# RMSNorm and swish: squares of three rows in one ScalarE operation, summed by one VectorE operation, eps on GpSimd

## The chip, the cores and the metric

The kernel runs on one core of a Trainium2 chip. The metric is the device time of a run in microseconds (us); medians of several runs are given. The profiled span is about 1.9 us shorter than that time (161.1 against 163.01 in the kernel before). All runs told of here are in the same, fast state, with a granted clock of 1.0. The experiments ran in three sets on three chips, and the kernel before ran beside each set (medians 163.10, 163.04 and 163.09 us); so between sets the ratio to the kernel before is compared, and not a few tenths of a us.

## The reference

```python
batch, seq, dim = 16, 1024, 512          # x: float32, gamma: ones, eps: 1e-5
rms = np.sqrt(np.mean(x ** 2, axis=-1, keepdims=True) + eps)
x_norm = x / rms * gamma
return (x_norm * (1.0 / (1.0 + np.exp(-x_norm)))).astype(np.float32)
```

There are 16384 rows of 512 numbers: 33.55 MB come in and 33.55 MB go out.

## The kernel before

Rows lie 128 at a time on the partitions. A chunk is four rows per partition (128x2048 numbers, 1 MB); there are 32 chunks in 11 tiles, and one tile is one load and one store of 4, 8 or 16 rows per partition. The ring holds 96 rows, so most loads are asked for long before the data is used.

```python
sizes = [4, 4, 8] + [16] * 6 + [8, 8];  ring = 96;  cn = 4;  n_act = 3

def sums(k):                    # sum of squares of each row
    for j in range(cn):
        row = xb[:, chunks[k] + j, :]
        if j < n_act:           # three rows on ScalarE
            nc.scalar.activation(out=junk[:], in_=row, func=AF.Square,
                                 accum_out=ms[:, k, j : j + 1])
        else:                   # the fourth on VectorE
            nc.vector.tensor_tensor_reduce(out=junk[:], in0=row, in1=row, ...,
                                           accum_out=ms[:, k, j : j + 1])
def root(k):                    # (sum / 512 + eps) ** -0.5
    nc.vector.tensor_scalar(out=aeps[:, k, :], in0=ms[:, k, :], scalar1=inv_d, scalar2=eps_f, ...)
    nc.gpsimd.tensor_tensor(out=rstd[:, k, :], in0=aeps[:, k, :], in1=neg_half[:], op=ALU.pow)
def norm(k):                    # four VectorE operations of 128x512, in place
    ...
def swish(k):                   # one Silu of 128x2048 on ScalarE, in place
    ...
for k in range(K + 3):          # order of issue on every engine
    sums(k); root(k); (store of a tile whose chunks are all <= k-3); norm(k - 1); swish(k - 2); (loads)
```

(Cut: `...`, the names of the junk tiles, and the bounds on k.)

## Time and profile before

| | before |
|---|---|
| time, median (range) | 163.01 us (162.89 to 163.02) |
| span | 161.1 us |
| busy: VectorE, ScalarE, GpSimd | 110.7, 118.7, 46.4 us |
| moved | 67.1 MB, 417 GB/s over the span |
| last store issued | at 146.8 us |

The lines, and how they are read, are in the prediction.

### The profile page before, as it was taken

To read this page: it belongs to the slowest core of one execution; us is meant where nothing else is said; L and a number is where in the kernel's file an instruction comes from. 1 tells how busy PE (TensorE), PEld (TensorE's weight loads), DVE (VectorE), ACT (ScalarE), POOL (GpSimd) and SP (SyncE) were. 2 spreads that over 40 slices of the span, in tenths; PEclk is the share of its full clock that TensorE was granted. 3 is DMA by queue.
4 is the path that set the end of the run, shared out by engine and by line. 5 is a ranking of instruction groups with operands and counts; after the bars stand their busy time and mean duration, and the time that the engine had idled before them with its cause. 6 is when DMAs were issued, how large, how long until landed. Compare 5 with 4: busy or idle time off the path is not lost.

```text
span 161.1 us, 612 instructions
## 1 busy us (share of the span) xinstructions
DVE 110.7 (69%) x226; ACT 118.7 (74%) x225; POOL 46.4 (29%) x38
## 2 busy tenths in 40 slices
DVE  0376946998999999999966998069999604990000
ACT  3447919999999999999939996099999408954000
POOL 1052403333444433333333333033333302400000
DMA  5999989999899999999999999999999999999993
GB/s 171 437 435 521 390 352 488 413 403 480 366 407 431 484 411 447 399 456 447 399 447 456 399 439 464 417 415 421 431 435 464 419 403 472 415 415 423 439 415 146
DMA packets 3180, 67.15 MB, mean 417 GB/s; under 512 B 356, under 2 KB 356, under 8 KB 360
## 3 DMA queue, kind: packets, MB, share of 16 engines
q1 hardware_dynamic: 1584, 33.56, 49.1%
q10 hardware_dynamic: 1592, 33.56, 48.4%
q14 instruction: 4, 0.03, 0.0%
HBM read 33.56 MB, written 33.55 MB: 417 GB/s over the span
## 4 chain that ended last, share of the span: by engine, by line
DMA 59%; ACT 20%; another core or an unknown queue 4%; issue 4%; DVE 3%; SPq 1%; DVEq 0%; ACTq 0%
DMA xb<-in_x_dram 41%; DMA out_dram<-xb 19%; ACT junk_a L80 12%; ACT xb L111 8%; DVE xb L104 3%; SPq L70 1%; DVEq L178 0%; DVE aeps L93 0%; ACTq L80 0%
## 5 line engine op out<-in xcount | busy, mean ns | idle before, releaser
L104 DVE SCALAR_TENSOR_TENSOR xb<-xb,rstd,gamma_sb 128x512 f32<-128x512 f32 x128 | 87.4, 745 | 0.0
L80 ACT ACTIVATE junk_a<-xb 128x512 bf16<-128x512 f32 x96 | 59.0, 615 | 23.9 <-DMA xb<-in_x_dram 23.9
L97 POOL TENSOR_TENSOR rstd<-aeps,neg_half 128x4 f32<-128x4 f32 x32 | 45.6, 1426 | 94.1 <-DVE aeps L93 94.1
L111 ACT ACTIVATE xb<-xb 128x2048 f32<-128x2048 f32 x32 | 60.7, 1896 | 1.8 <-DVE xb L104 1.8
L86 DVE CUSTOM_DVE_ANT_0 junk_v<-xb 128x512 bf16<-128x512 f32 x32 | 21.9, 685 | 19.6 <-DMA xb<-in_x_dram 19.6
L80 ACT ACTIVATION_READ_ACCUMULATOR junk_a<-xb 128x1 f32 x96 | 18.0, 187 | 0.0
L93 DVE TENSOR_SCALAR aeps<-ms 128x4 f32<-128x4 f32 x32 | 5.4, 170 | 14.5 <-ACT junk_a L80 14.5
L117 ACT ACT_TABLE_LOAD x1 | 1.3, 1283 | 2.4 <-issue 2.4
L86 DVE DVE_READ_ACCUMULATOR2_ANT ms<- 128x1 f32 x32 | 2.6, 82 | 0.0
L140 DVE STREAM_SHUFFLE gamma_sb<-gamma 128x512 f32<-128x512 f32 x1 | 0.7, 725 | 0.0
L114 POOL MEMSET gamma<- 128x512 f32 x1 | 0.5, 524 | 0.3 <-POOLq L164 0.3
L164 POOL MEMSET const-float32-0.0<- 128x1 f32 x1 | 0.1, 98 | 0.2 <-issue 0.2
L164 POOL MEMSET const-bfloat16-1.0<- 128x1 bf16 x1 | 0.1, 101 | 0.0
L164 POOL MEMSET const-uint8-127<- 128x1 uint8 x1 | 0.1, 101 | 0.0
L115 POOL MEMSET neg_half<- 128x4 f32 x1 | 0.1, 101 | 0.0
L164 POOL MEMSET const-float32-1.0<- 128x1 f32 x1 | 0.1, 98 | 0.0
L140 DVE LOAD_MASK_SELECT gamma_sb<-gamma x1 | 0.0, 14 | 0.0
## 6 DMA issues: line engine op xcount, KB each, us to landing
xb<-in_x_dram SPq DMA_DIRECT2D x6, 4096.0 KB, 43.8
out_dram<-xb ACTq DMA_DIRECT2D x6, 4096.0 KB, 34.6
xb<-in_x_dram SPq DMA_DIRECT2D x3, 2048.0 KB, 38.8
out_dram<-xb ACTq DMA_DIRECT2D x3, 2048.0 KB, 13.9
xb<-in_x_dram SPq DMA_DIRECT2D x2, 1024.0 KB, 5.8
out_dram<-xb ACTq DMA_DIRECT2D x2, 1024.0 KB, 19.7
gamma<-in_gamma_dram ACTq DMA_DIRECT2D x1, 8.0 KB
```

The costliest lines, as they stand in the source:

```text
L70: nc.sync.dma_start(out=buf(t), in_=dram(xf, t))
L80: nc.scalar.activation(out=junk[:], in_=row, func=AF.Square, accum_out=ms[:, k, j : j + 1],)
L86: nc.vector.tensor_tensor_reduce(out=junk[:], in0=row, in1=row, scale=1.0, scalar=0.0, op0=ALU.mult, op1=ALU.add, accum_out=ms[:, k, j : j ...
L93: nc.vector.tensor_scalar(out=aeps[:, k, :], in0=ms[:, k, :], scalar1=inv_d, scalar2=eps_f, op0=ALU.mult, op1=ALU.add,)
L97: nc.gpsimd.tensor_tensor(out=rstd[:, k, :], in0=aeps[:, k, :], in1=neg_half[:], op=ALU.pow)
L104: nc.vector.scalar_tensor_tensor(out=row, in0=row, scalar=rstd[:, k, j : j + 1], in1=gamma_sb[:], op0=ALU.mult, op1=ALU.mult,)
L111: nc.scalar.activation(out=rows, in_=rows, func=AF.Silu)
L114: nc.gpsimd.memset(gamma4[:], 0.0)
L115: nc.gpsimd.memset(neg_half[:], -0.5)
L117: nc.scalar.preload_act_table_set("silu_and_others")
L140: nc.vector.stream_shuffle(gamma_sb[:], gamma4[:], [0] * 32)
L164: nc = _bacc.Bacc("TRN2", target_bir_lowering=False, num_devices=1)
```

## The change

The intent is to take fixed costs away: three squares of 615 ns become one operation, their three accumulator reads of 187 ns become one VectorE sum, and the small operation with eps (170 ns) leaves VectorE. (In the kernel before a ScalarE operation on 512 elements lasts 615 ns and one on 2048 lasts 1896; the straight line through the two has some 190 ns left at 0 elements.) In exchange ScalarE takes over the fourth row, and the factor 1/512 moves into the scale of the squares. The diff is shortened, with `...` for what was cut; the pool `squares_pool` and `at = chunks[k]` are set up above it.

```diff
 def sums(k):
-    for j in range(cn):
-        ... Square with accumulator on ScalarE (j < 3), square-and-sum on VectorE (j = 3)
+    sq = squares_pool.tile([P, n_sq, D], fp32, name="sq")        # PSUM, two buffers, n_sq = 3
+    nc.scalar.activation(out=sq[:], in_=xb[:, at : at + n_sq, :], func=AF.Square, scale=inv_d**0.5)
+    for j in range(n_sq, cn):                                    # the fourth row
+        nc.scalar.activation(out=junk[:], in_=xb[:, at + j, :], func=AF.Square,
+                             scale=inv_d**0.5, accum_out=ms[:, k, j : j + 1])
+    nc.vector.tensor_reduce(out=ms[:, k, 0:n_sq], in_=sq[:], op=ALU.add, axis=X)
 def root(k):
-    nc.vector.tensor_scalar(out=aeps[:, k, :], in0=ms[:, k, :], scalar1=inv_d, scalar2=eps_f, ...)
+    nc.gpsimd.tensor_scalar(out=aeps[:, k, :], in0=ms[:, k, :], scalar1=eps_f, op0=ALU.add)
     nc.gpsimd.tensor_tensor(out=rstd[:, k, :], in0=aeps[:, k, :], in1=neg_half[:], op=ALU.pow)
```

More of the change, by code (lines that the diff above doesn't have):

```diff
@@ L33 @@
     cn = 4
-    n_act = 3
+    n_sq = 3
     N = sum(sizes)
@@ L48 @@
     pool = ctx.enter_context(tc.tile_pool(name="all", bufs=1))
+    squares_pool = ctx.enter_context(
+        tc.tile_pool(name="squares", bufs=2, space=bass.MemoryType.PSUM)
+    )
     junk_pool = ctx.enter_context(tc.tile_pool(name="junk", bufs=1))
@@ L75, in sums @@
     def sums(k):
-        for j in range(cn):
-            row = xb[:, chunks[k] + j, :]
-            if j < n_act:
-                junk = junk_pool.tile([P, D], bf16, name=f"junk_a{j}")
-                nc.scalar.activation(
-                    out=junk[:], in_=row, func=AF.Square,
-                    accum_out=ms[:, k, j : j + 1],
-                )
-            else:
-                junk = junk_pool.tile([P, D], bf16, name=f"junk_v{j}")
-                nc.vector.tensor_tensor_reduce(
-                    out=junk[:], in0=row, in1=row,
-                    scale=1.0, scalar=0.0, op0=ALU.mult, op1=ALU.add,
-                    accum_out=ms[:, k, j : j + 1],
-                )
+        at = chunks[k]
+        sq = squares_pool.tile([P, n_sq, D], fp32, name="sq")
+        nc.scalar.activation(
+            out=sq[:], in_=xb[:, at : at + n_sq, :], func=AF.Square,
+            scale=inv_d**0.5,
+        )
+        for j in range(n_sq, cn):
+            junk = junk_pool.tile([P, D], bf16, name=f"junk_a{j}")
+            nc.scalar.activation(
+                out=junk[:], in_=xb[:, at + j, :], func=AF.Square,
+                scale=inv_d**0.5, accum_out=ms[:, k, j : j + 1],
+            )
+        nc.vector.tensor_reduce(
+            out=ms[:, k, 0:n_sq], in_=sq[:], op=ALU.add,
+            axis=mybir.AxisListType.X,
+        )
     def root(k):
-        nc.vector.tensor_scalar(
-            out=aeps[:, k, :], in0=ms[:, k, :], scalar1=inv_d, scalar2=eps_f,
-            op0=ALU.mult, op1=ALU.add,
+        nc.gpsimd.tensor_scalar(
+            out=aeps[:, k, :], in0=ms[:, k, :], scalar1=eps_f, scalar2=None,
+            op0=ALU.add,
         )
```

## The prediction

> **What bounds the kernel now.** I read the page from the top: busy shares, the row of slices, the chain that ended last, the groups; then the stretches at the end and the timeline of one steady chunk. A chunk is 4 rows per partition (128x2048 elements, 1 MB); there are 32 of them, in 11 tiles.
>
> ```profile
> span 161.1 us, 612 instructions
> DVE 110.7 (69%) x226; ACT 118.7 (74%) x225; POOL 46.4 (29%) x38
> DMA  5999989999899999999999999999999999999993
> HBM read 33.56 MB, written 33.55 MB: 417 GB/s over the span
> DMA xb<-in_x_dram 41%; DMA out_dram<-xb 19%; ACT junk_a L80 12%; ACT xb L111 8%; DVE xb L104 3%; SPq L70 1%; DVEq L178 0%; DVE aeps L93 0%; ACTq L80 0%
> ...
> L104 DVE SCALAR_TENSOR_TENSOR xb<-xb,rstd,gamma_sb 128x512 f32<-128x512 f32 x128 | 87.4, 745 | 0.0
> L80 ACT ACTIVATE junk_a<-xb 128x512 bf16<-128x512 f32 x96 | 59.0, 615 | 23.9 <-DMA xb<-in_x_dram 23.9
> L97 POOL TENSOR_TENSOR rstd<-aeps,neg_half 128x4 f32<-128x4 f32 x32 | 45.6, 1426 | 94.1 <-DVE aeps L93 94.1
> L111 ACT ACTIVATE xb<-xb 128x2048 f32<-128x2048 f32 x32 | 60.7, 1896 | 1.8 <-DVE xb L104 1.8
> L86 DVE CUSTOM_DVE_ANT_0 junk_v<-xb 128x512 bf16<-128x512 f32 x32 | 21.9, 685 | 19.6 <-DMA xb<-in_x_dram 19.6
> ```
>
> The reader sees a DMA row at 9 in nearly every slice but the first and the last, while no engine is over 74% busy and both VectorE and ScalarE end their idle time by waiting for loads (19.6 and 23.9 us). The kernel moves 67.1 MB; that is the bound. The windows of the end, with the columns window, length, busy time and count of DVE, ACT, POOL, clock, DMA share, GB/s:
>
> ```profile
> 61.00:105.00 44.00, 34.70 (x72) 35.77 (x69) 14.39 (x10) 1.00 1.00 433
> 134.00:147.00 13.00, 9.26 (x18) 10.93 (x16) 2.88 (x2) 1.00 1.02 441
> 147.00:161.10 14.10, 0.00 (x0) 0.00 (x0) 0.00 (x0) 1.00 0.79 339
> ```
>
> The transfers run at about 433 GB/s to the end, and the last 14.1 us hold no compute at all: the last store is issued at 146.8 us and then only the queue of stores drains. So compute could end later without moving the end, by an amount that I work out below. It is the number on which this case turns.
>
> The timeline of a steady chunk, start and length in us:
>
> ```profile
> 43.74 1.90 ACT L111 ACTIVATE xb<-xb 128x2048 f32<-128x2048 f32 x1
> ...
> 47.38 1.90 ACT L111 ACTIVATE xb<-xb 128x2048 f32<-128x2048 f32 x1
> ```
>
> From one Silu to the next it is 3.64 us: ScalarE sets the pace of compute where loads are there. The DMA needs 2.1 MB per chunk, read and written, or 4.84 us at 433 GB/s, so compute is 1.2 us per chunk ahead of the DMA.
>
> [...] In the trace the square-and-sum of 512 lasts 685 ns but its accumulator read starts 0.61 us after it[...]. No PSUM operand is in this trace. [...] All 128 normalizations last 743 to 752 ns, most power operations beside them: VectorE, at least, pays nothing here. [...]
>
> **The change part by part, for one chunk.**
>
> ScalarE. Removed: three squares of 512 with accumulator reads, which pace at 0.61 us each (from the timeline: 42.52, 43.13, 43.74), 1.84 us. Added: one square of 1536, [...] 1.37 us, and one square with accumulator, 0.61 us: 1.98 us. With the Silu at 1.80 us of pace the chunk is 3.78 us against 3.64: ScalarE gets 0.14 us slower, since it takes over the fourth row and saves only two fixed costs. [...]
>
> VectorE. Removed: the square-and-sum (0.61 us of pace plus 0.08 for its read) and the mean-plus-eps of 0.09 us pace: about 0.78 us. Added: one sum of 3x512 from PSUM, [...] I take 1.72 us. Staying: four normalizations, each 0.66 us after the one before (two of them, 745 ns long, merge to 1.41 us), 2.65 us. Sum: 2.65 + 1.72 = 4.37 us, against 3.43 before. **VectorE replaces ScalarE as the pace of compute**, with 32 x 4.37 = 140 us of a 161 us span. But 4.37 is still under the 4.84 us of the DMA.
>
> GpSimd. Added: an addition of eps on 128x4; no such row exists, so I bound it by the power's 1.43 us. From the end of a chunk's sum to its first normalization VectorE does four normalizations and a sum in the new order of instructions (2.65 + 1.72 = 4.37 us). Two GpSimd operations and their signals take at most 2 x 1.43 + some 0.3 = 3.2 us. It fits, 1.2 us to spare. The scale of 1/512 folded into the square is free.
>
> DMA: the same loads and stores in the same order.
>
> **Does the slower VectorE reach the end?** Tile 3 lands at 23.6 us (the timeline shows ScalarE starting chunk 4 at 23.70), so chunk 4's sum starts at 23.7 + 1.4 = 25.1 us. From there VectorE runs 4.37 us per chunk: later loads landed at 84.5 (chunk 20), 104.8 (24) and 133.7 (30), and the sums of these chunks start at 95.0, 112.5 and 138.7, so it never waits for a load again. Then:
> - sum of chunk 31 starts at 25.1 + 27 x 4.37 = 143.1, two chunks' normalization follow: 143.1 + 1.7 + 2 x 2.65 = 150.1, the last Silu 1.9: last store issued at 152.0 us instead of 146.8.
> - Silu of chunk 27, which releases tile 8's store: the sum of 28 starts at 130.0, + 1.7 + 2.65 + 1.9 = 136.3 us (before: 133.9).
>
> How late may they be? After 134 us the windows show 13.0 x 441 + 14.1 x 339 = 10.5 MB. The three last stores are 8.4 MB of these, so 2.1 MB of older stores remain at 134 and last till 134 + 4.9 = 138.9. Tile 8's store needs its first bytes by then: 136.3 + about 1.5 = 137.8. Margin 1 us. The last store (2.1 MB) is reached at 134 + 19.4 = 153.4; its first bytes come at 152.0 + 1.5 = 153.5. Margin none. (The 1.5 is an estimate: a 1 MB load took 4.8 us from issue to landing, of which 2.4 are transfer at 433 GB/s, the other 2.4 lie ahead and behind.) So the span should just hold, 161 to 161.5, and the time with it, 163.2 us. Every 0.05 us on VectorE's chunk beyond this adds 27 x 0.05 = 1.4 us.
>
> **The rivals.**
> 1. The sum costs more than 1.72 us[...]. Then VectorE is the bound: at 1.80 the last store is 2 us late and the time about 165, at 1.90 about 167.5. For it: no row of the kernel measures it. [...]
> 2. GpSimd takes over: if addition and power need over 4.3 us, each chunk is longer by the excess, some 2.8 us per 0.1. For it: the power is already 1.43 us for 4 elements. Against: the first power, before any normalization, took only 1.01.
> 3. Compute gets faster and the kernel with it: nothing speaks for it. Even free compute leaves 67.1 MB at 433 GB/s, 155 us, plus the first landing and the last receipt; the DMA row has no gap to fill.
> 4. Fully hidden[...]: 163.0.
>
> **Range and chances.** Rivals 4 and the middle case give 163.0 to 163.5 (some 70%); a reduction 0.05 to 0.1 us slower gives 164 to 166 (20%); the rest is worse. Faster by 2% would need under 159.8: 1%. Slower by 2% is over 166.3, a chunk of about 4.5 us: 9%. Range 162.6 to 165.6, point 163.2.
>
> **What would show it.** VectorE busy about 142 us and with hardly any idle time after chunk 4; the sum's row at 1.7 to 1.8 us; ScalarE waiting about 0.6 us per chunk for normalizations instead of for loads; the last store issued near 152 us; the DMA row at 9 until the last slices. Wrong, if the DMA row thins out after slice 33, or if the normalization waits for GpSimd.

Passages that no trace or run of this case shows are cut, with the cut marked, and terms of the forecast's sum are among them: how the 1.37 us of the square of 1536 and the 1.72 us of the sum were come by. The sum came to 2.65 + 1.72 = 4.37 us for VectorE's chunk and 1.37 + 0.61 + 1.80 = 3.78 us for ScalarE's, and from 4.37 to a last store at 152.0 us and a time of 163.2 us. The 1.37 can be had from the trace: the straight line through 615 ns at 512 elements and 1896 at 2048 gives 1469 ns at 1536, less the 0.10 us by which a Silu's length (1.90) is above its pace (1.80). For the 1.72 there is nothing of the kind, since no row of the kernel before reads PSUM or sums as many elements: it was the author's estimate. So were the some 0.3 us for GpSimd's signals; the timeline of the changed kernel below has 0.16 us from the end of the sum to the addition and 0.09 us from the addition to the power. That the scale is free is what the run shows: squares of 512 last 613 ns with it and 615 without. That the transfers can't go above 433 GB/s was not shown.

## The result, and the profile after

The changed kernel took 162.64 us (162.43 to 162.95), against 163.01 of the kernel before: ratio 0.9981, 95% interval 0.9962 to 0.9999. (A ratio is the mean time of one kernel's fast runs over that of the other's fast runs of the same rounds, so it is not quite the ratio of the medians.)

The page of the changed kernel: busy time, the DMA row, the chain that ended last by engine, and the groups (operation, shapes, count, busy us, mean ns, idle time before and what ended it).

```profile
DVE 139.1 (86%) x162; ACT 126.2 (78%) x129; POOL 63.2 (39%) x70
DMA  5999989899899999999999999899999999999994
DVE 74%; DMA 13%; issue 2%; ACT 2%; SPq 1%; DVEq 1%
...
L108 DVE SCALAR_TENSOR_TENSOR xb<-xb,rstd,gamma_sb 128x512 f32<-128x512 f32 x128 | 87.2, 743 | 0.0
L115 ACT ACTIVATE xb<-xb 128x2048 f32<-128x2048 f32 x32 | 61.1, 1909 | 14.1 <-DVE xb L108 14.0
L91 DVE TENSOR_REDUCE ms<-sq 128x3 f32<-128x1536 f32 x32 | 56.0, 1749 | 9.5 <-ACT sq L81 9.4
L81 ACT ACTIVATE sq<-xb 128x1536 f32<-128x1536 f32 x32 | 46.0, 1439 | 7.8 <-DMA xb<-in_x_dram 7.8
L97 POOL TENSOR_SCALAR aeps<-ms 128x4 f32<-128x4 f32 x32 | 18.4, 575 | 79.1 <-DVE ms L91 79.1
L101 POOL TENSOR_TENSOR rstd<-aeps,neg_half 128x4 f32<-128x4 f32 x32 | 44.0, 1376 | 2.7
```

VectorE grew by 28.4 us and ScalarE by 7.5 us, and the time did not follow: the DMA row is as full as before. ScalarE's waits for loads fell from 23.9 to 7.8 us, and a wait of 14.0 us for VectorE's normalizations took their place. The page's chain now names VectorE for 74% of the span. It follows the last store back through the chunks; whether that makes VectorE the bound is what the experiments ask.

The timeline of one chunk of the changed kernel (start, length, engine, operation):

```profile
42.27 1.75 DVE L91 TENSOR_REDUCE ms<-sq 128x3 f32<-128x1536 f32 x1
43.94 2.73 DVE L108 SCALAR_TENSOR_TENSOR xb<-xb,rstd,gamma_sb 128x512 f32<-128x512 f32 x4
44.18 0.58 POOL L97 TENSOR_SCALAR aeps<-ms 128x4 f32<-128x4 f32 x1 [2.26 <-DVE ms L91]
...
44.85 1.39 POOL L101 TENSOR_TENSOR rstd<-aeps,neg_half 128x4 f32<-128x4 f32 x1
...
46.59 1.75 DVE L91 TENSOR_REDUCE ms<-sq 128x3 f32<-128x1536 f32 x1
```

A chunk takes VectorE 46.59 - 42.27 = 4.32 us, without a gap: 1.67 from the start of the sum to the first normalization and 2.65 for the four. The windows of the end (columns as in the prediction):

```profile
134.00:147.00 13.00, 13.00 (x17) 9.75 (x10) 5.92 (x6) 1.00 1.03 444
147.00:160.90 13.90, 1.56 (x3) 2.77 (x2) 0.00 (x0) 1.00 0.80 342
```

Compute now reaches into the last stretch (1.56 and 2.77 us, where there was none), and the transfers move the same as before, 444 and 342 GB/s against 441 and 339. The last store was issued at 150.5 us instead of 146.8.

### The profile page after: what moved, and what is told of

Same layout as the page of the kernel before. It is cut to its first block, busy times and chain, and to the rows that moved or that the text cites. A ratio compares the mean times of both kernels' runs of the same rounds, so it can differ in the third digit from the quotient of the medians.

```text
span 160.9 us, 488 instructions
## 1 busy us (share of the span) xinstructions
DVE 139.1 (86%) x162; ACT 126.2 (78%) x129; POOL 63.2 (39%) x70
## 4 chain that ended last, share of the span: by engine, by line
DVE 74%; DMA 13%; issue 2%; ACT 2%; SPq 1%; DVEq 1%
DVE xb L108 45%; DVE ms L91 29%; DMA xb<-in_x_dram 13%; ACT xb L115 1%; ACT sq L81 1%; SPq L73 1%; DVEq L182 1%; DVEq L108 0%
## 5 line engine op out<-in xcount | busy, mean ns | idle before, releaser
L91 DVE TENSOR_REDUCE ms<-sq 128x3 f32<-128x1536 f32 x32 | 56.0, 1749 | 9.5 <-ACT sq L81 9.4
L81 ACT ACTIVATE sq<-xb 128x1536 f32<-128x1536 f32 x32 | 46.0, 1439 | 7.8 <-DMA xb<-in_x_dram 7.8
L97 POOL TENSOR_SCALAR aeps<-ms 128x4 f32<-128x4 f32 x32 | 18.4, 575 | 79.1 <-DVE ms L91 79.1
L101 POOL TENSOR_TENSOR rstd<-aeps,neg_half 128x4 f32<-128x4 f32 x32 | 44.0, 1376 | 2.7
L87 ACT ACTIVATE junk_a<-xb 128x512 bf16<-128x512 f32 x32 | 19.6, 613 | 0.0
L87 ACT ACTIVATION_READ_ACCUMULATOR junk_a<-xb 128x1 f32 x32 | 6.0, 186 | 0.0
```

What stands on the lines that cost most here:

```text
L81: nc.scalar.activation(out=sq[:], in_=xb[:, at : at + n_sq, :], func=AF.Square, scale=inv_d**0.5,)
L87: nc.scalar.activation(out=junk[:], in_=xb[:, at + j, :], func=AF.Square, scale=inv_d**0.5, accum_out=ms[:, k, j : j + 1],)
L91: nc.vector.tensor_reduce(out=ms[:, k, 0:n_sq], in_=sq[:], op=ALU.add, axis=mybir.AxisListType.X,)
L97: nc.gpsimd.tensor_scalar(out=aeps[:, k, :], in0=ms[:, k, :], scalar1=eps_f, scalar2=None, op0=ALU.add,)
```

## The experiments

**Theory A**: both kernels sit on the floor of the transfers, and compute may end later by a certain slack before the stores run dry. **Theory B**: the VectorE chain sets the end, as the chain's 74% suggests, and the gain elsewhere cancels the loss. **Theory C**: compute has ample room, whatever it costs. (The diffs are shortened: arguments and the new small tiles that they write to are left out.)

### Doses: one, two and four small VectorE operations more in each chunk

```diff
         nc.vector.tensor_reduce(out=ms[:, k, 0:n_sq], in_=sq[:], ...)
+        for i in range(n):                                        # n = 1, 2, 4
+            nc.vector.tensor_scalar(out=dose[:, k, i, :], in0=neg_half[:], scalar1=1.0, op0=ALU.add)
```

> The changed kernel with one extra VectorE operation on 128x4 per chunk, about 0.08 us, which nobody waits for. Theory A (DMA bound; compute may end 1.3 us later than the 150.5 us of the changed kernel before the stores run dry): VectorE's chunk 4.32 -> 4.40 us, last store issued at 150.5 + 27 x 0.08 = 152.7, time 162.6 + 0.9 = 163.5 us. Theory B (the VectorE chain that the changed kernel's page names for 74% of the span sets the end): the whole 27 x 0.08 = 2.2 us is added, 164.8. Theory C (DMA alone, compute has ample room): 162.6.

> The same with two extra operations, about 0.16 us per chunk. A: last store at 154.9, of which 1.3 us are absorbed, time 162.6 + 3.1 = 165.7. B: 162.6 + 4.4 = 167.0. C: 162.6.

> The same with four, about 0.33 us per chunk. A: last store at 159.5, time 162.6 + 7.6 = 170.2; the slope between two and four is the full 27 us per us of chunk. B: 162.6 + 8.9 = 171.5. C: 162.6.

Two lines of the timeline with one dose, and the DMA rows with two and with four doses:

```profile
101.62 0.16 DVE L97 TENSOR_SCALAR dose<-neg_half 128x4 f32<-128x4 f32 x1
101.69 2.73 DVE L114 SCALAR_TENSOR_TENSOR xb<-xb,rstd,gamma_sb 128x512 f32<-128x512 f32 x4
```

```profile
DMA  5999989999999999999999999999999999899966
```

```profile
DMA  5999998999999999989999999999999995597965
```

A dose costs 101.69 - 101.62 = 0.07 us. With two doses the DMA row opens at its end, with four its last seven slices read 5, 5, 9, 7, 9, 6, 5: the stores run dry. The next table has the last store's issue (from the stores' own view), the span, and what lies between them.

| kernel | compute's chunk, us | last store issued | span | from it to the end | time, us | ratio to before |
|---|---|---|---|---|---|---|
| before | 3.64 (ScalarE) | 146.8 | 161.1 | 14.3 | 163.01 | 1 |
| changed | 4.32 (VectorE) | 150.5 | 160.9 | 10.4 | 162.64 | 0.9981 |
| one dose | 4.39 | 152.9 | 161.5 | 8.6 | 163.24 | 1.0011 |
| two doses | 4.46 | 154.8 | 162.0 | 7.2 | 163.76 | 1.0037 |
| four doses | 4.60 | 158.6 | 165.8 | 7.2 | 167.67 | 1.0283 |

B is refuted: two doses put the last store off by 4.3 us and cost 1.1. C is refuted: four doses cost 5.0. (By the ratios, which allow for the two sets, it is 0.9 and 4.9.) A holds, with a larger slack than expected: it had said 163.5, 165.7 and 170.2 us. With two and four doses the last store needs the same 7.2 us to the end, so there it runs alone and sets the end. The knee follows: the changed kernel's span, 160.9, less 7.2 is 153.7, which is 3.2 us after its own last store. Beyond it every microsecond counts in full: from two to four doses the store moves by 3.8 us and the span by 3.8. On the near side the store can move freely: in two profiles told of below (the change once more, and twice the power) it is issued at 152.0, and the spans are 161.0 and 160.9.

How do the 7.2 us come about, and how did the full queue end in the kernel before? The windows, columns as in the prediction, first of two doses from the issue of the last store, then of the kernel before:

```profile
154.83:155.67 0.84, 0.00 (x0) 0.00 (x0) 0.00 (x0) 1.00 0.00 0
155.67:160.75 5.08, 0.00 (x0) 0.00 (x0) 0.00 (x0) 1.00 0.98 413
160.75:161.99 1.24, 0.00 (x0) 0.00 (x0) 0.00 (x0) 1.00 0.00 0
```

```profile
147.00:158.00 11.00, 0.00 (x0) 0.00 (x0) 0.00 (x0) 1.00 0.98 420
158.00:161.10 3.10, 0.00 (x0) 0.00 (x0) 0.00 (x0) 1.00 0.13 53
```

The lone store needs 0.84 us to its first packet, 5.08 to move 2.1 MB, and 1.24 to the end. The full queue runs at 420 GB/s up to 158 us; the 339 of the whole stretch is an average with an end in which little moves.

One dose has its last store 0.8 us before the knee, yet took 163.24 us, 0.4 to 0.6 more than the changed kernel (162.64, and 162.80 when it was run once more); from the kernel before, run beside it, it can't be told apart (ratio 0.9995 to 1.0027). The times of single packets in the traces, which no view prints, show what these profiled spans differ by. A store ends with sixteen packets of 4 bytes. In the changed kernel fifteen of them come by 159.1 us and the last at 159.6; with one dose fifteen by 158.9 and the last at 160.2, and the span is 0.6 us longer. The end of the store before was already 0.6 us late (155.35 against 154.76), and the eps part alone, whose last store is issued as early as 147.0, shows the same (160.5 at the end, span 161.8). So it is not shown that the late store costs the one dose anything; why one packet lags is open.

### Faster compute: two rows squared into PSUM instead of three

```diff
-    n_sq = 3
+    n_sq = 2
```

> The changed kernel with two rows squared into PSUM and two summed on ScalarE. VectorE's chunk falls[...] to 3.78, ScalarE's is then some 3.9 to 4.0. A: compute is faster and the time is not, 162.5 to 163.1, with waits for loads back. B: VectorE's chain falls by 27 x 0.35 = 9 us, time about 153.

(The term by which VectorE's chunk was to fall to 3.78 us is cut; it was an estimate.) The sum's row fell from 1749 to 1225 ns, and its pace from 1.67 to 1.14 us (100.41 to 101.55 us in its timeline). The time: 162.96 us (162.81 to 163.16), ratio 0.9989 (0.9974 to 1.0003). The page's chain by engine, and its DMA row:

```profile
DMA  5999989999999999999999999999999999998993
...
DMA 40%; ACT 39%; issue 5%; another core or an unknown queue 3%; DVE 3%; SPq 1%; DVEq 1%
```

The stores show 3.97 us per chunk (63.76 to 79.64 us for four chunks), 0.35 less than the changed kernel, and the last store at 146.6. VectorE's share of the chain fell from 74% to 3% and the time did not move. So that 74% was a chain of work that happened to run without waiting, not the bound. B would have had 153 us.

### The floor: loads, Silu and stores alone

```diff
-            if k < K:
-                sums(k)
-                root(k)
 ...
-            if 1 <= k <= K:
-                norm(k - 1)
```

> Wrong result on purpose: loads, Silu and stores alone, no squares, sums, powers or normalizations. Theory A (both kernels sit on the floor of the transfers): 162.4 to 163.1 us. Rival (compute still costs some us at the start or the end, or slows the transfers): 155 to 160.

The result is wrong, as meant. 162.30 us (161.96 to 162.62), ratio 0.9953 (0.9939 to 0.9966). Its busy row, DMA row and the Silu's group:

```profile
DVE 0.7 (0%) x2; ACT 60.1 (38%) x33; POOL 0.8 (0%) x6
...
DMA  5999899899999999999999999999999999999895
...
L115 ACT ACTIVATE xb<-xb 128x2048 f32<-128x2048 f32 x32 | 58.8, 1898 | 84.5 <-DMA xb<-in_x_dram 84.5
```

Taking away nearly all of VectorE's and GpSimd's work and half of ScalarE's saves 0.5%. With these transfers that bounds what a change of the squares, sums, powers and normalizations could win here; the Silu was not taken away.

### The squares part alone: eps stays on VectorE

```diff
-        nc.gpsimd.tensor_scalar(
+        nc.vector.tensor_scalar(
             out=aeps[:, k, :], in0=ms[:, k, :], scalar1=eps_f, scalar2=None,
```

> The changed kernel with the addition of eps left on VectorE: the squares part of the change alone. VectorE gets back an operation of 0.07 us of pace, and it has to wait for the end of its own sum before it (1.75 us long, 1.67 of pace) and for the signal, some 0.1 to 0.2 us more: chunk 4.32 -> 4.49 to 4.59 us, last store issued at 155.1 to 157.8. Theory A with the slack that the doses showed (about 3.1 us of delay absorbed): 162.6 + 1.5 to 4.2 = 164 to 167 us. Rival (moving eps to GpSimd is of no account): 162.6.

168.16 us (168.03 to 168.28), ratio 1.0313 (1.0299 to 1.0326): 1.2 us over the upper end of what A expected. One chunk in the timeline:

```profile
99.26 1.75 DVE L91 TENSOR_REDUCE ms<-sq 128x3 f32<-128x1536 f32 x1
...
101.12 0.17 DVE L97 TENSOR_SCALAR aeps<-ms 128x4 f32<-128x4 f32 x1
...
101.19 2.73 DVE L108 SCALAR_TENSOR_TENSOR xb<-xb,rstd,gamma_sb 128x512 f32<-128x512 f32 x4
...
103.84 1.75 DVE L91 TENSOR_REDUCE ms<-sq 128x3 f32<-128x1536 f32 x1
```

The small operation starts 1.86 us after the sum's start, 0.11 us after its end, where a dose that needs nothing of the sum starts after 1.67 (99.95 to 101.62 us with one dose). So reading the sum's own result costs 0.19 us more than its 0.07 of pace. The chunk is 4.58 us here (4.62 the next), 0.26 to 0.30 more than in the changed kernel; the last store is issued at 159.2, 1.4 us after the latest that was expected, and the span is 166.4: again 7.2 us between. The squares part alone is therefore 3% slower than the kernel before, and moving eps to GpSimd is what keeps the whole change within the slack.

### The eps part alone, and the change once more

```diff
# the kernel before
     def root(k):
-        nc.vector.tensor_scalar(
+        nc.gpsimd.tensor_scalar(
```

> The kernel before with eps alone moved to GpSimd: the other part of the change by itself. VectorE loses an operation it did not wait for long, GpSimd gets 0.6 us per chunk, ScalarE's chunk stays 3.64 us. Theory A: the floor of the transfers, 162.5 to 163.1, as before. Rival (the small gain of the changed kernel comes from this part): 0.998 of the kernel before, as the changed kernel had.

> The changed kernel once more, beside the kernel before and eps_pool on the same chip. If the 0.2% by which it was ahead is its own, the ratio is 0.997 to 0.999 again; if it was chance, 1.000 lies inside the interval. Theory A expects no more than the distance to the floor of loads, Silu and stores alone, 0.5%.

The eps part alone: 163.16 us (163.06 to 163.55), ratio 1.0004 (0.9989 to 1.0019), no effect. The changed kernel again: 162.80 us (162.37 to 163.18), ratio 0.998 (0.9962 to 0.9997). With 0.9981 in the first runs and 0.9976 in the run with two powers (below) the 0.2% is likely its own, and it does not come from the eps part alone; it is inside the 0.5% to the floor. Where it comes from stays open. The profiled runs show only where it sits: the last packet of the last store comes at 159.9 us in the kernel before, at 159.6 and 159.7 in the two profiles of the changed kernel, and at 158.8 in the floor run, and the span ends 1.2 to 1.3 us later in each.

This second profile of the changed kernel showed something else. From 91.8 us on, in all 13 chunks that were left, GpSimd's addition lasted not 0.59 but 2.58 us:

```profile
87.49 0.59 POOL L97 TENSOR_SCALAR aeps<-ms 128x4 f32<-128x4 f32 x1 [2.26 <-DVE ms L91]
88.16 1.39 POOL L101 TENSOR_TENSOR rstd<-aeps,neg_half 128x4 f32<-128x4 f32 x1
91.80 2.58 POOL L97 TENSOR_SCALAR aeps<-ms 128x4 f32<-128x4 f32 x1 [2.26 <-DVE ms L91]
94.46 1.04 POOL L101 TENSOR_TENSOR rstd<-aeps,neg_half 128x4 f32<-128x4 f32 x1
```

It lasts about as long as the four normalizations beside it (2.65 us), and the power after it, now beside a sum, is as short (1.04 us) as the first power of the changed kernel, which ran before any normalization (1.04 us). GpSimd's 2.0 us of room (below) took it up. Only the last chunk waited, 1.2 us, and the last store came at 152.0: no sum lies between the last two chunks' normalizations, so that the room there is only 0.3 us (in the first profile the last power is done at 145.49 and VectorE comes to its result at 145.83). Why the addition went over to 2.58 us stays open.

### Twice the power on GpSimd

```diff
+        nc.gpsimd.tensor_tensor(out=spare[:, k, :], in0=aeps[:, k, :], in1=neg_half[:], op=ALU.pow)
         nc.gpsimd.tensor_tensor(out=rstd[:, k, :], in0=aeps[:, k, :], in1=neg_half[:], op=ALU.pow)
```

> The changed kernel with a second power on GpSimd ahead of the real one, 1.39 us on the way from a chunk's sum to its normalization. In the changed kernel's trace GpSimd is done at 46.24 us and the normalization starts at 48.26, so 2.0 us are free there. Theory A: 0.6 us stay free, VectorE's chunk unchanged, 162.6. Rival (GpSimd is close behind VectorE, or its reads hold VectorE up): the chunk grows by 0.3 us or more, time 167 or more.

162.80 us (162.39 to 163.01), ratio 0.9976 (0.9959 to 0.9993). One chunk:

```profile
101.40 1.39 POOL L102 TENSOR_TENSOR spare<-aeps,neg_half 128x4 f32<-128x4 f32 x1
...
102.77 1.32 POOL L105 TENSOR_TENSOR rstd<-aeps,neg_half 128x4 f32<-128x4 f32 x1
...
104.80 2.73 DVE L112 SCALAR_TENSOR_TENSOR xb<-xb,rstd,gamma_sb 128x512 f32<-128x512 f32 x4
```

The real power is done at 104.09 and the normalization starts at 104.80, on VectorE's own pace: 0.7 us are still free. The normalizations last 743 ns on the mean, as in the changed kernel, so the second power does not hold VectorE up. Again only the last chunk waited for GpSimd, 0.9 us, and the last store came at 152.0. GpSimd is not behind the time of the changed kernel.

### A try at the transfers: first tiles of 8 rows

```diff
-    sizes = [4, 4, 8] + [16] * 6 + [8, 8]
+    sizes = [8, 8] + [16] * 6 + [8, 8]
```

> The changed kernel with tiles of 8, 8 rows at the start instead of 4, 4, 8: no packets of 8 KB, one load and one store less. In the changed kernel's trace the stretch from 20 to 25 us, where the first stores of 8 KB packets run, moved 394 GB/s instead of 430, that is some 0.4 us lost. Theory A: the gain is at most that, 162.2 to 162.8; the later first chunk (3 us) costs part of the 3.1 us slack and nothing else. Rival (compute sets the end): 3 us more.

162.80 us (162.52 to 163.39), ratio 0.9989 (0.9972 to 1.0007): no gain to be told from chance. (The trace of the changed kernel reads 401 GB/s from 20 to 25 us, not 394, and 422 from 25 to 60: there was less to win than was expected.) No correct version beat both kernels.

## Why the prediction was right

- **The number**: in the range, but only just. 162.64 us lies 0.04 above its lower end of 162.6, two of the four runs (162.51 and 162.43) lie below it, and the point of 163.2 was 0.6 too high. The prediction's likeliest case had the time stay or rise by up to 0.3%; it fell by 0.2%, which nothing in it explains. The mechanism was right; that the number fell inside the range was in part luck.
- **The DMA as the bound**: right. The floor of loads, Silu and stores is 162.30 us, so both kernels are within 0.5% of it.
- **VectorE replaces ScalarE as the pace of compute**: right. 4.32 us against 4.37 predicted. The term that was a little large is the sum: 1.67 us of pace instead of 1.72. The 1.72 was an estimate that no row of the kernel before bore out, so its being close was partly luck. VectorE was busy 139.1 us (about 142 said) and waited only 9.5 us, all at the start.
- **ScalarE**: right. Its new square has a pace of 1.38 us (44.20 to 45.58 us in its timeline) against 1.37; it lasts 1439 ns, 30 less than the straight line through the lengths of the kernel before gives, and why is not shown. The scale is free: its squares of 512 last 613 ns with it and 615 without. It waits 0.42 us in a steady chunk for normalizations (0.6 said).
- **The last store's issue**: 150.5 us against 152.0 said; tile 8's store at 134.9 against 136.3. The difference is mostly the sum's 0.05 us over 24 to 27 chunks.
- **GpSimd fits**: right, with more room in a steady chunk than said: the addition took 0.58 us, not the 1.43 that bounded it. But it can take 2.58, as the second profile shows, which the bound did not cover, and the prediction overlooked the last chunk, where no sum stands between and the room is 0.3 us. (The first addition of the changed kernel, before any normalization, took 0.23 us; the normalizations' mean is 743 ns in both profiles.)
- **"Margin none" for the last store**: here sizes were wrong. By the prediction the last store may be issued at 153.4 - 1.5 = 151.9 us at the latest; by the runs it is 153.7. That the queue reaches the last store at 153.4 was right: in the kernel before, its first packets run at 153.6. The time from issue to first bytes was too large, 0.84 us and not 1.5. The remaining 1.1 us I put down to the spread of the sixteen last packets: the last one of the store before came only at 154.8 us in the changed kernel (155.0 in the kernel before), and the last one of the last store came 4.8 to 4.9 us after it (159.6 and 159.9). With the 1.4 us by which the store itself came earlier than 151.9, the slack was 3.2 us. "Every 0.05 us on VectorE's chunk adds 1.4 us" therefore holds only past the knee: the two doses that lead from two to four, 0.14 us, cost 3.9.
- **The chance of slower**: real. The squares part alone, with some 0.3 us more per chunk, took 168 us; a sum that much costlier would likely have made the change slower by about as much.

## What to carry to other kernels

When transfers are the bound, as here, a change of compute is judged by when the last store is issued, not by busy time: find how long a lone last store needs to the end (here 7.2 us), subtract it from the span, and compare with the issue. An engine that the chain names for three quarters of the span may cost nothing at all (here 74%, and the time did not fall when it was 3%: 162.64 and 162.96 us); add a small dose to it and see. Before moving work onto an engine that will become the pace, count also the waits for its own results (here 0.19 us in a chunk), which do not show in the busy time of any row.
